# The down projection of a decoder layer: 16 of its 22 row tiles by Strassen's method with seven products

## The chip, the core and the metric

The kernel runs on one core of a Trainium2 chip. A core has five engines with instruction streams of their own: TensorE (PE, matrix products into PSUM), VectorE (DVE), ScalarE (ACT), GpSimd (POOL) and SyncE (SP), which here only issues transfers. Transfers between HBM and the on-chip SBUF run on 16 DMA engines; SP and ACT feed them through hardware queues, POOL through a software queue. The metric is the device time of one execution in microseconds (us). A run is compared with runs of the kernel before on the same chip.

## The reference, cut to what matters

The layer computes attention, a state space branch, a merge and a first layer norm; all of that is untouched. Behind it comes this, for 512 tokens, a width of 1024 and an inner width of 2816 (float32):

```
h = _layer_norm(DN_ALPHA * h + mixed @ w_o[i], ln1_g[i], ln1_b[i])
up = _causal_dwconv(h @ w_up[i], conv_w[i], conv_b[i])
val, gate = up[..., :D_FF], up[..., D_FF:]
ffn = (jax.nn.silu(gate) * val) @ w_down[i]
ple = (p[i] @ w_pe[i]) * jax.nn.sigmoid(h @ w_pe_gate[i])
h = _layer_norm(DN_ALPHA * h + ffn + ple, ln2_g[i], ln2_b[i])
```

## The kernel before, in words

Every float32 operand of a large product is split into a high part (a cast to the format that TensorE takes, by ACT) and a low part (operand minus high part, by DVE). `mm3` then makes one product of three matmuls: high by high, high by low, low by high, each with a 128x128 stationary operand and up to 512 moving columns.

SBUF is managed as pages of 128 partitions by 1024 floats (4 KB each). `Pages` hands them out in the order in which they came free, so a page's new user waits for the last reader of the old one. `Weights` streams 128 weight pages through them: SP loads a raw page (`wr`), ACT makes `wh`, DVE makes `wl`, and the raw page is freed. `use(n)` makes sure that the splits are issued one page ahead and the loads three pages ahead. The code is written in program order; a scheduler then places each instruction on its engine's queue, and the queues run strictly in order.

`ffn_up` runs over 22 feature tiles `f`. For each it makes two groups of 24 matmuls (value and gate, banks `up`), ACT and DVE apply the convolution (`cv`, one ACT activation and two DVE operations for each), ACT the SiLU, DVE the product, and the result is split into a page `act{f}`.

`ffn_down` multiplies these 22 pages by the 22 pages of `w_down`. Its eight banks (4 token tiles by 2 halves of 512 columns) accumulate over the first 16 row tiles in an order in which each weight page serves 24 matmuls. For the last 6 row tiles the order is by bank, so that each token tile ends in turn, is added to the residual `res`, normalized and stored while TensorE is at the next one.

Of the kernel before, what the change touches and what calls it, by code (L numbers as in the profile page):

```python
# [29 lines left out]
NPAGES, NHALVES = 37, 6  # L30
NPAGES_LATE = 11
LAG_B, LAG_C = 5, 7
# [52 lines left out]
class Weights:  # L85


    def __init__(self, tc, pages, srcs, fetch_ahead=FETCH_AHEAD, split_ahead=SPLIT_AHEAD):
# [5 lines left out]
    @staticmethod  # L94
    def cuts(n):
        return [slice(0, 512), slice(512, 1024)] if n == 0 else [slice(0, 1024)]

# [70 lines left out]


class Layer:  # L170
    def __init__(self, tc, cst, pages, banks, a):
        self.tc, self.nc, self.cst, self.pages, self.banks, self.a = tc, tc.nc, cst, pages, banks, a
        srcs = []

        def add(name):
            base = len(srcs)
            ap = a[name]
            srcs.extend(ap[i] for i in range(ap.shape[0]))
            return base

        self.wuv = add("w_uv")
        self.wqk = add("w_qk")
# [7 lines left out]
        self.wdn = add("w_down")  # L190
        self.W = Weights(tc, pages, srcs)


# [46 lines left out]
    def constants(self):  # L240
        nc, cst = self.nc, self.cst
        self.small_idx = {}
        self.small_buf = cst.tile([P, 28, 16], F32, name="small_buf")
        self.pair_idx = {}
        self.pair_buf = cst.tile([P, 16, 2, 16], F32, name="pair_buf")
# [9 lines left out]
        self.tri = cst.tile([P, 2, P], F32R, name="tri")  # L255
# [5 lines left out]
        self.mask = cst.tile([P, 2, P], F32R, name="mask")  # L261
# [323 lines left out]
    def ssm_load(self):  # L585
# [4 lines left out]
        for g in range(2):  # L590
            nc.sync.dma_start(self.lst[64 * g:64 * g + 64], a["log_step"][g:g + 1].to_broadcast([64, 16]))
        self.d32 = self.cst.tile([32, 16], F32, name="d32")
        nc.sync.dma_start(self.d32, a["d"])
# [10 lines left out]

        self.dec = [self.cst.tile([P, 2, P], F32, name=f"dec{i}") for i in range(2)]
        for dec in self.dec:
            nc.gpsimd.memset(dec[:, :, 0:1], 0.0)
        self.Tf = [self.cst.tile([P, 4, P], F32, name=f"Tf{i}") for i in range(2)]
        for tf in self.Tf:
# [59 lines left out]
    def ssm_prep(self):  # L669
# [13 lines left out]

        self.dd = self.cst.tile([32, 16, 32], F32, name="dd")
        self.tt_wide(self.dd, self.ident[0:32, 0:32].unsqueeze(1).to_broadcast([32, 16, 32]),
# [307 lines left out]

    def bcast_load(self, name, tag):
        pg = self.pages.get(tag)
        self.nc.gpsimd.dma_start(pg.t, self.a[name].to_broadcast([P, DM]))
        return pg
# [123 lines left out]
    def ffn_up(self):  # L1121
        nc = self.nc
        self.act = []
        for f in range(NF):
# [16 lines left out]
            yp.free()  # L1141
            self.act.append(pg)
            yield
        for pg in self.hT:
            pg.free()

    def load_conv(self):
# [4 lines left out]


    def ffn_down(self):
        nc, W = self.nc, self.W
        g2 = self.bcast_load("ln2_g", "g2")
        b2 = self.bcast_load("ln2_b", "b2")
        bk = {(t, h): self.banks.get(f"d{t}{h}") for t in range(4) for h in range(2)}
        KO = NF - 6
        for k in range(KO):  # L1160
            w = W.use(self.wdn + k)
            for t in range(4):
                for h in range(2):
                    self.token_mms(bk[t, h], self.act[k], t, h, w, k, k == 0, False)
            W.free(self.wdn + k)
            self.act[k].free()
        ws = [W.use(self.wdn + k) for k in range(KO, NF)]
        halves = (slice(0, 512), slice(512, 1024))

        q = slice(768, 1024)  # L1170
        self.tt(self.res[3].t[:, q], self.res[3].t[:, q], bk[3, 1].t[:, 256:512], ALU.add)
        for t in range(4):
            r = self.res[t].t
            parts = [(c, bk[t, i].t, False) for i, c in enumerate(halves)]
            if t == 3:
                parts[1:] = [(slice(512, 768), bk[3, 1].t[:, 0:256], False), (q, bk[0, 0].t[:, 0:256], True)]
            st, mv = self.ln_tiles(len(parts))
            ts_ = slice(t * P, t * P + P)
            for i, (c, bank, fresh) in enumerate(parts):
                for k in range(KO, NF):  # L1180
                    a, w = self.act[k].t, ws[k - KO]
                    self.mm3(bank, a[:, 0, ts_], a[:, 1, ts_], w[0].t[:, c], w[1].t[:, c],
                             fresh and k == KO, k == NF - 1)
                self.tt(r[:, c], r[:, c], bank, ALU.add)
# [114 lines left out]
def layouts(i):  # L1299
# [18 lines left out]
        "w_up": up,  # L1318
        "w_down": _rows(i["w_down"][0], 1),
        "a_re": state(i["ssm_a_re"][0]),  # L1320
# [32 lines left out]
```

## Time and profile before

| what | value |
|---|---|
| median of 3 runs | 802.91 us (802.33 to 803.2) |
| profiled execution: its time | 802.31 us |
| profiled execution: its span, first to last instruction | 800.6 us |
| time around the span (difference) | 1.71 us |
| mean granted TensorE clock | 0.997 of full speed |

The profile is of one execution. Its span is what the trace's rows add up to; the device time holds 1.71 us more. Times of a row count from the start of the span.

### The profile page before, as it was taken

Reading aid. Unit: us, or ns where it says so; the run is one execution under the profiler, and the core shown is the slowest. Engines: PE = TensorE matmul, PEld = TensorE weight load, DVE = VectorE, ACT = ScalarE, POOL = GpSimd, SP = SyncE. Lnnn points to the kernel's source line nnn. Section 1 sums busy time; section 2 is a strip of 40 time slices with the busy share of each in tenths; the row PEclk is TensorE's granted clock in tenths of the full one; section 3 lists DMA queues with packets and bytes.
Section 4 is the critical chain, followed back from the end, with each engine's and each line's share of the span. In section 5 each row is a group of like instructions: output and inputs, shape, how many; then the busy total and the mean of one; then the engine's idle time right before and its main releaser. Section 6 shows DMA issues by size and latency. Waiting matters only on the chain.

```text
span 800.6 us, 9760 instructions
## 1 busy us (share of the span) xinstructions
PE 784.6 (98%) x3716; PEld 655.8 (82%) x3716; DVE 508.2 (63%) x881; ACT 333.1 (42%) x538; POOL 24.2 (3%) x67
## 2 busy tenths in 40 slices
PE   9999999999999999999999999999999999999996
PEld 7887888878888878888888888888888888888885
DVE  6957997695767868857644665565555565432056
ACT  7435667553433375415323443444344345312000
POOL 0000000000000010013300000000000000000000
PEclk9999999999999999999999999999999999999998
DMA  8913221033122475515203322312222126431002
GB/s 319 379 70 103 56 80 54 27 107 131 35 71 91 173 237 170 187 42 180 80 27 132 106 79 79 105 52 94 93 79 79 53 90 252 158 105 53 1 27 79
DMA packets 29870, 86.73 MB, mean 108 GB/s; under 512 B 4224, under 2 KB 8448, under 8 KB 29568
## 3 DMA queue, kind: packets, MB, share of 16 engines
q1 hardware_dynamic: 27952, 80.35, 29.5%
q0 software_dynamic: 1296, 4.72, 1.6%
q10 hardware_dynamic: 576, 1.05, 0.3%
q8 instruction: 29, 0.48, 0.2%
q14 instruction: 17, 0.14, 0.0%
HBM read 79.81 MB, written 3.15 MB: 104 GB/s over the span
## 4 chain that ended last, share of the span: by engine, by line
PE 92%; DVE 3%; ACT 2%; DMA 2%; issue 1%; SPq 1%; DVEq 0%; ACTq 0%
PE up L195 30%; PE d L195 15%; PE g L195 10%; PE o L195 5%; PE pg L195 5%; PE mx L195 4%; PE z L195 3%; PE u L195 3%; PE v L195 3%; PE kb L195 2%; PE qb L195 2%; PE A L195 2%; PE pe L195 1%; PE y L195 1%; DMA y<-yst 1%; PE av L195 1%
## 5 line engine op out<-in xcount | busy, mean ns | idle before, releaser
L120 DVE TENSOR_TENSOR wl<-wr,wh 128x1024 fp32r<-128x1024 f32 (+1 forms) x129 | 155.1, 1214 | 100.0 <-ACT wh L119 82.6
L195 PE MATMUL up<-hT,wh 128*128 128x512 f32 x704 | 216.7, 389 | 0.0
L119 ACT CAST wh<-wr 128x1024 fp32r<-128x1024 f32 (+1 forms) x129 | 133.3, 1043 | 149.8 <-PE d L195 38.1
L195 PEld LDWEIGHTS up<-hT,wh 128*128 128x128 f32 x704 | 132.2, 188 | 27.5
L195 PE MATMUL up<-hT,wl 128*128 128x512 f32 x352 | 136.9, 389 | 0.0
L195 PE MATMUL d<-wh,act 128*128 128x512 f32 (+1 forms) x364 | 109.1, 382 | 0.0
L225 DVE SCALAR_TENSOR_TENSOR cv<-up,cw,cv 128x511 f32<-128x511 f32 x88 | 65.8, 748 | 32.2 <-ACT cv L1133 30.7
L195 PE MATMUL g<-xs,wh 128*128 128x512 f32 x256 | 81.0, 397 | 0.0
L195 PEld LDWEIGHTS d<-wh,act 128*128 128x128 f32 x364 | 67.6, 188 | 13.3
L195 PEld LDWEIGHTS up<-hT,wl 128*128 128x128 f32 x352 | 66.1, 188 | 13.6
L195 PE MATMUL d<-wl,act 128*128 128x512 f32 (+1 forms) x182 | 69.5, 382 | 0.0
L1133 ACT ACTIVATE cv<-up,cb,cw 128x512 f32<-128x512 f32 x44 | 34.2, 778 | 58.5 <-PE up L195 58.5
L195 PEld LDWEIGHTS g<-xs,wh 128*128 128x128 f32 x256 | 46.2, 188 | 8.6 <-issue 0.6
L195 PE MATMUL g<-xs,wl 128*128 128x512 f32 x128 | 50.0, 391 | 0.0
L195 PE MATMUL mx<-yts,wh 128*128 128x512 f32 x128 | 39.2, 390 | 1.4 <-DVE yts L903 1.4
L195 PE MATMUL pg<-wh,hT 128*128 128x512 f32 x128 | 40.1, 390 | 0.0
L195 PE MATMUL o<-wh,mx 128*128 128x512 f32 x128 | 40.0, 390 | 0.0
L195 PEld LDWEIGHTS d<-wl,act 128*128 128x128 f32 x182 | 34.2, 188 | 6.6
L216 DVE TENSOR_TENSOR cv<-cv 128x512 f32<-128x512 f32 x22 | 15.2, 692 | 24.6 <-ACT cv L232 24.6
L195 PEld LDWEIGHTS mx<-yts,wh 128*128 128x128 f32 x128 | 24.0, 188 | 6.7 <-DVE yts L903 1.8
L216 DVE TENSOR_TENSOR x<-x,d 128x512 f32<-128x512 f32 (+1 forms) x10 | 6.1, 606 | 35.1 <-PE d L195 35.1
L195 PEld LDWEIGHTS g<-xs,wl 128*128 128x128 f32 x128 | 24.0, 188 | 5.2
(180 smaller groups left out, 1143.3 us busy)
## 6 DMA issues: line engine op xcount, KB each, us to landing
wr<-in_w_up_dram SPq DMA_DIRECT2D x44, 512.0 KB, 3.3
wr<-in_w_down_dram SPq DMA_DIRECT2D x22, 512.0 KB, 3.4
wr<-in_w_g_dram SPq DMA_DIRECT2D x16, 512.0 KB, 3.3
wr<-in_w_qk_dram SPq DMA_DIRECT2D x8, 512.0 KB, 11.3
wr<-in_w_glu_dram SPq DMA_DIRECT2D x8, 512.0 KB, 4.3
wr<-in_w_o_dram SPq DMA_DIRECT2D x8, 512.0 KB, 3.9
wr<-in_w_pe_gate_dram SPq DMA_DIRECT2D x8, 512.0 KB, 3.3
wr<-in_w_uv_dram SPq DMA_DIRECT2D x7, 512.0 KB, 7.7
```

The costliest lines, as they stand in the source:

```text
L119: self.nc.scalar.copy(hi.t[:, c], raw.t[:, c])
L120: self.nc.vector.tensor_tensor(out=lo.t[:, c], in0=raw.t[:, c], in1=hi.t[:, c].bitcast(F32), op=ALU.subtract)
L195: ins = self.nc.tensor.matmul(out=out, lhsT=lhsT, rhs=rhs, start=start, stop=stop, skip_group_check=True).ins
L216: return self.nc.vector.tensor_tensor(out=out, in0=a, in1=b, op=op).ins
L225: self.nc.vector.scalar_tensor_tensor(out=out, in0=a, scalar=s, in1=b, op0=op0, op1=op1)
L1133: nc.scalar.activation(y, bank.t, AF.Identity, scale=cw[:, 2:3], bias=cb)
```

## The change

The first 16 of the 22 row tiles of `w_down` are taken as two block rows (even and odd tiles), the 1024 output columns as two block columns, and the 512 tokens as two block rows of the activations. The four blocks of this product are made by seven block products instead of eight (Winograd's form of Strassen's method), each over 8 row tiles, 2 token tiles and 512 columns: 48 matmuls. The last 6 row tiles stay as they were, through a `Weights` stream of their own (`WD`).

The activation sums are made by DVE in `ffn_up` (`combine`, tiles of 256 tokens); four of the seven left operands are split there, and three (`S1`, `A12`, `S4`) are kept as sums and split in `ffn_down` (`split_left`). The weight sums are made in `Products`: a block page is loaded by SP (16 pages), negated in place by ACT, and a second block is added by a transfer from HBM that accumulates into the page (`accum_op`), issued by POOL. Of the 28 pages (7 products by 4), the pages 4 to 7, 8 to 11, 12 to 15 and 16 to 19 need such a step; pages 8 to 11 are made from 4 to 7 and 12 to 15 from 8 to 11, in the same buffers (`dr4` to `dr7`), and 16 to 19 from `dr0` to `dr3`. Then `dh` (ACT) and `dl` (DVE) are split from the page as before. A page of weights now serves 12 matmuls.

Around it: the late page pool has 14 pages instead of 11 (tables of the state space branch move to a pool that is closed by then), and the loads of `ln2_g` and `ln2_b` move from POOL's queue to SP's.

```diff
-NPAGES_LATE = 11
+NPAGES_LATE = 14
+NS = 8
...
+class Products:
+    ORDER = (("11", None, 0),
+             ("22", None, "12"),
+             ("-T3", 1, "11"),
+             ("T2", 2, "21"),
+             ("11", 0, "12"),
+             ("21", None, 0),
+             ("22", None, 0))
+    KEPT = (0, 1, 2)
+    def __init__(self, tc, pages, blocks, fetch_ahead=5, split_ahead=1):
...
+    def fetch_to(self, n):
+        while self.nf < min(n, self.n):
+            q, j = divmod(self.nf, self.per)
+            name, of, plus = self.ORDER[q]
+            if of is None:
+                pg = self.pages.get(f"dr{self.nf}")
+                self.nc.sync.dma_start(pg.t, self.block(name, j))
+            else:
+                pg = self.raw.pop((of, j))
+            if plus:
+                self.nc.scalar.mul(pg.t, pg.t, -1.0)
+                self.nc.gpsimd.dma_start(pg.t, self.block(plus, j), accum_op=ALU.add)
+            self.raw[q, j] = pg
+            self.nf += 1
+    def split_to(self, n):
...
+            self.nc.scalar.copy(hi.t, raw.t)
+            self.nc.vector.tensor_tensor(out=lo.t, in0=raw.t, in1=hi.t.bitcast(F32), op=ALU.subtract)
+            if q not in self.KEPT:
+                self.raw.pop((q, j)).free()
...
@@ ffn_up
-            self.tt(yp.t[:, 0], yp.t[:, 0], yp.t[:, 1], ALU.mult)
-            pg = self.pages.get(f"act{f}", F32R, (P, 2, T))
-            self.split(pg.t[:, 0], pg.t[:, 1], yp.t[:, 0])
+            if f < 2 * NS:
+                self.combine(f, yp)
...
+            if f >= NF - 2:
+                self.WP.split_to(f - NF + 3)
+                self.WP.fetch_to(f - NF + 4)
@@ combine (odd tile of a pair)
+        self.tt(a12, y0[:, first], y1[:, first], ALU.mult)
+        self.tt(sq[:, 3], y0[:, last], y1[:, last], ALU.mult)
+        self.tt(sq[:, 1], a21, sq[:, 0], ALU.subtract)
+        self.tt(s1, a21, sq[:, 3], ALU.add)
+        self.tt(sq[:, 2], s1, sq[:, 0], ALU.subtract)
+        self.tt(s4, a12, sq[:, 2], ALU.subtract)
+        for i in range(2):
+            pg = self.pages.get(f"sa{p}{i}", F32R, (P, 2, 2, T // 2))
+            src = sq[:, 2 * i:2 * i + 2]
+            nc.scalar.copy(pg.t[:, :, 0], src)
+            self.tt(pg.t[:, :, 1], src, pg.t[:, :, 0].bitcast(F32), ALU.subtract)
@@ ffn_down
-        for k in range(KO):
-            w = W.use(self.wdn + k)
-            for t in range(4):
-                for h in range(2):
-                    self.token_mms(bk[t, h], self.act[k], t, h, w, k, k == 0, False)
+        def product(q, bank, a, fresh, side=lambda j: None):
...
+                for k in range(2):
+                    p = 2 * j + k
+                    for m in range(2):
+                        ts_ = slice(m * P, m * P + P)
+                        self.mm3(bank[m].t, a[p][0][:, ts_], a[p][1][:, ts_], hi[:, k], lo[:, k],
+                                 fresh and p == 0, p == NS - 1)
...
+        product(0, X, now(0, 0), True)
+        add(X, 0, 0)
+        product(1, Y, now(0, 1), True)
+        add(Y, 1, 1)
+        product(2, X, now(1, 0), False)
+        add(X, 1, 0)
+        a = left("S1")
+        product(3, Y, now(1, 1), False)
+        product(4, X, a, False)
+        add(X, 1, 1)
+        product(5, V, left("A12"), True)
+        product(6, X, left("S4"), False, lambda j: WD.use(j))
```

Three places of the built programs matter for what follows. The first is ACT's queue where the up projection ends and the down projection begins. In the kernel before it holds, beside the last convolution (`cv21`), SiLU and the split of `act21`, only casts of weight pages:

```order
L1133 ACTIVATE cv21_5466<-up211_5501,cb_314,cw_313 128x512
L119 CAST wh109_5612<-wr109_5556 128x1024
L119 CAST wh112_5702<-wr112_5646 128x1024
L232 ACTIVATE cv21_5466<-cv21_5466 128x512
L119 CAST wh110_5642<-wr110_5586 128x1024
L212 CAST act21_5537<-cv21_5466 128x512
```

In the changed kernel the same stretch reads as follows (L207 is the negation, L219 the cast of a weight page):

```order
L219 CAST dh3_5650<-dr3_5608 128x1024
L1200 ACTIVATE cv21_5534<-up211_5567,cb_314,cw_313 128x512
L207 ACTIVATE dr6_5634<-dr6_5634 128x1024
L207 ACTIVATE dr7_5654<-dr7_5654 128x1024
L207 ACTIVATE dr3_5608<-dr3_5608 128x1024
L207 ACTIVATE dr4_5610<-dr4_5610 128x1024
L299 ACTIVATE cv21_5534<-cv21_5534 128x512
L207 ACTIVATE dr5_5614<-dr5_5614 128x1024
L279 CAST act21_5597<-cv21_5534 128x512
L219 CAST dh6_5710<-dr6_5634 128x1024
L219 CAST dh2_5630<-dr2_5604 128x1024
L219 CAST dh7_5728<-dr7_5654 128x1024
```

The cast of page 2 (`dh2`), which product 0 takes third, now stands behind five negations, the SiLU, the split of `act21` and the cast of page 6 (`dh6`), which needs that page's accumulating transfer.

The second place is POOL's queue. Before, its last two entries are the loads of `ln2_g` and `ln2_b`:

```order
L996 DMA g2_5540<-in_ln2_g_dram 128x1024
L996 DMA b2_5542<-in_ln2_b_dram 128x1024
```

Now it ends with the 16 accumulating transfers, of which these are the second to the tenth:

```order
L208 DMA dr1_5532<-in_w_down_blocks_dram 128x1024
L208 DMA dr6_5634<-in_w_down_blocks_dram 128x1024
L208 DMA dr7_5654<-in_w_down_blocks_dram 128x1024
L208 DMA dr3_5608<-in_w_down_blocks_dram 128x1024
L208 DMA dr4_5610<-in_w_down_blocks_dram 128x1024
L208 DMA dr5_5614<-in_w_down_blocks_dram 128x1024
L208 DMA dr6_5634<-in_w_down_blocks_dram 128x1024
L208 DMA dr2_5604<-in_w_down_blocks_dram 128x1024
L208 DMA dr4_5610<-in_w_down_blocks_dram 128x1024
```

So pages 1 and 3 (used only as pages 17 and 19, in product 4) are summed ahead of or between the pages of product 1.

The third place is SP's queue behind the last page of `w_up`. Before, 22 pages of `w_down` follow in it; now eight block pages do, with `dr6` and `dr7` ahead of `dr4` and `dr5`, then the two loads that left POOL:

```order
L203 DMA dr2_5604<-in_w_down_blocks_dram 128x1024
L203 DMA dr3_5608<-in_w_down_blocks_dram 128x1024
L203 DMA dr6_5634<-in_w_down_blocks_dram 128x1024
L203 DMA dr7_5654<-in_w_down_blocks_dram 128x1024
L203 DMA dr4_5610<-in_w_down_blocks_dram 128x1024
L203 DMA dr5_5614<-in_w_down_blocks_dram 128x1024
L1063 DMA b2_5842<-in_ln2_b_dram 128x1024
L1063 DMA g2_5840<-in_ln2_g_dram 128x1024
```

## Rows read from the trace of the kernel before

**Rows 1.** The page, parts 1 and 2: busy time by engine; transfer rate in 40 slices.

```profile
PE 784.6 (98%) x3716; PEld 655.8 (82%) x3716; DVE 508.2 (63%) x881; ACT 333.1 (42%) x538; POOL 24.2 (3%) x67
...
GB/s 319 379 70 103 56 80 54 27 107 131 35 71 91 173 237 170 187 42 180 80 27 132 106 79 79 105 52 94 93 79 79 53 90 252 158 105 53 1 27 79
```

**Rows 2.** The chain that ended last, from 640 us: start, length, what, count.

```profile
639.96 32.87 PE up L195 x145
672.83 119.92 PE d L195 x546
...
796.74 0.66 DVEq L1349
```

**Rows 3.** TensorE's matmuls from 672 us by shape: count, busy, mean ns.

```profile
L195 PE MATMUL d<-wh,act 128*128 128x512 f32 x340 | 104.8, 389 | 0.0
L195 PE MATMUL d<-wl,act 128*128 128x512 f32 x170 | 66.1, 389 | 0.0
```

**Rows 4.** Busy time by stretch: length, busy (instructions) by engine, clock, DMA, GB/s.

```profile
450.00:665.00 215.00, 215.00 (x951) 178.07 (x950) 125.40 (x154) 88.22 (x115) 1.13 (x2) 1.00 0.25 85
665.00:740.00 75.00, 75.00 (x333) 62.12 (x332) 30.51 (x29) 25.96 (x28) 0.00 (x0) 1.00 0.41 144
```

**Rows 5.** Who waited for whom from 660 us: in total, times, longest.

```profile
ACT wh L119 <- PE d L195: 38.1, 9, 4.6
```

**Rows 6.** ACT by line and shape, whole span: count, busy, mean ns, idle before.

```profile
L119 ACT CAST wh<-wr 128x1024 fp32r<-128x1024 f32 x127 | 132.0, 1050 | 148.0 <-PE d L195 38.1 <-DMA wr<-in_w_up_dram 18.2 <-PE o L195 15.6
L1133 ACT ACTIVATE cv<-up,cb,cw 128x512 f32<-128x512 f32 x44 | 34.2, 778 | 58.5 <-PE up L195 58.5
L232 ACT ACTIVATE cv<-cv 128x512 f32<-128x512 f32 x22 | 13.9, 631 | 26.8 <-DVE cv L225 26.8
L212 ACT CAST act<-cv 128x512 fp32r<-128x512 f32 x22 | 13.7, 621 | 15.2 <-DVE cv L216 15.2
...
L232 ACT ACTIVATE gate<-gate 128x1024 f32<-128x1024 f32 x8 | 7.8, 1046 | 0.0
```

**Rows 7.** DVE by line and shape, whole span: count, busy, mean ns.

```profile
L120 DVE TENSOR_TENSOR wl<-wr,wh 128x1024 fp32r<-128x1024 f32 x127 | 153.7, 1222 | 99.0 <-ACT wh L119 81.7 <-PE d L195 9.3 <-PE up L195 7.6
...
L216 DVE TENSOR_TENSOR cv<-cv 128x512 f32<-128x512 f32 x22 | 15.2, 692 | 24.6 <-ACT cv L232 24.6
...
L216 DVE TENSOR_TENSOR vx<-pq 128x256 f32<-128x256 f32 x16 | 6.1, 422 | 0.1
```

**Rows 8.** DMA issues by line: count, KB each, median us from issue to landing.

```profile
wr<-in_w_down_dram SPq DMA_DIRECT2D x22, 512.0 KB, 3.4
...
x<-in_x_dram POOLq DMA_DIRECT2D x4, 512.0 KB, 5.4
...
praw<-in_pT_dram POOLq DMA_DIRECT2D x1, 512.0 KB, 11.9
```

**Rows 9.** Timeline of POOL, 275 to 300 us: start, length, what, count.

```profile
279.21 2.29 POOL L1010 DMA_DIRECT2D x<-in_x_dram  x4 [3.83 <-DVE yts L216]
...
282.53 0.53 POOL L1016 DMA_DIRECT2D praw<-in_pT_dram  x1
```

**Rows 10.** Landing of the four transfers into `x` on POOL's queue.

```profile
DMA to landing us min/median/max: 3.8/5.4/7.4
```

**Rows 11.** TensorE's longest waits in the whole span: in total, times, longest.

```profile
PE z L195 <- ACT wp L232: 2.0, 3, 1.6
PE mx L195 <- DVE yts L903: 1.4, 1, 1.4
```

**Rows 12.** Busy time by stretch at the very end, columns as in rows 4.

```profile
793.00:796.00 3.00, 0.00 (x0) 0.00 (x0) 2.79 (x10) 0.29 (x1) 0.00 (x0) 1.00 0.00 0
796.00:800.60 4.60, 0.00 (x0) 0.00 (x0) 1.41 (x2) 0.00 (x0) 0.00 (x0) 0.55 0.30 114
```

More of the change, by code (lines that the diff above doesn't have):

```diff
@@ L92, in __init__, with cuts @@
         self.nf = self.ns = 0
-    @staticmethod
-    def cuts(n):
-        return [slice(0, 512), slice(512, 1024)] if n == 0 else [slice(0, 1024)]
+    def cuts(self, n):
+        return [slice(0, 512), slice(512, 1024)] if n == 0 and self.halved else [slice(0, 1024)]
     def fetch_to(self, n):
@@ L189, in __init__ @@
         self.wup = add("w_up")
-        self.wdn = add("w_down")
         self.W = Weights(tc, pages, srcs)
+        self.WD = Weights(tc, pages, [a["w_down"][i] for i in range(NF - 2 * NS)], halved=False)
+        self.WP = Products(tc, pages, a["w_down_blocks"])
     def mm(self, out, lhsT, rhs, start, stop):
@@ L1122, in ffn_up @@
         nc = self.nc
-        self.act = []
+        self.act, self.left, self.now = [], {}, ([], [])
         for f in range(NF):
@@ L1145, in ffn_up, with combine @@
             pg.free()
+    def combine(self, f, yp):
+        nc, p = self.nc, f // 2
+        first, last = slice(0, T // 2), slice(T // 2, T)
+        y0, y1 = yp.t[:, 0], yp.t[:, 1]
+        if f % 2 == 0:
+            self.sq = self.pages.get(f"sq{p}", F32, (P, 4, T // 2))
+            self.tt(self.sq.t[:, 0], y0[:, first], y1[:, first], ALU.mult)
+            self.tt(y0[:, last], y0[:, last], y1[:, last], ALU.mult)
+            self.even = yp
+            return
+        sq, q = self.sq.t, p % 4
+        if q == 0:
+            for name in ("S1", "A12", "S4"):
+                self.left.setdefault(name, []).append(self.pages.get(f"{name}{p}", F32, (P, 4, T // 2)))
+        s1, a12, s4 = (self.left[name][-1].t[:, q] for name in ("S1", "A12", "S4"))
+        a21 = self.even.t[:, 0, last]
+        self.tt(a12, y0[:, first], y1[:, first], ALU.mult)
+        self.tt(sq[:, 3], y0[:, last], y1[:, last], ALU.mult)
+        yp.free()
+        self.tt(sq[:, 1], a21, sq[:, 0], ALU.subtract)
+        self.tt(s1, a21, sq[:, 3], ALU.add)
+        self.even.free()
+        self.tt(sq[:, 2], s1, sq[:, 0], ALU.subtract)
[5 more added lines that the diff above has]
+            self.tt(pg.t[:, :, 1], src, pg.t[:, :, 0].bitcast(F32), ALU.subtract)
+            self.now[i].append(pg)
+        self.sq.free()
     def load_conv(self):
@@ L1151, in load_conv, with split_left @@
         self.nc.sync.dma_start(self.cb, self.a["conv_b"])
-    def ffn_down(self):
[L1155 to L1159, printed above, removed]
-        for k in range(KO):
-            w = W.use(self.wdn + k)
-            for t in range(4):
-                for h in range(2):
-                    self.token_mms(bk[t, h], self.act[k], t, h, w, k, k == 0, False)
-            W.free(self.wdn + k)
-            self.act[k].free()
-        ws = [W.use(self.wdn + k) for k in range(KO, NF)]
-        halves = (slice(0, 512), slice(512, 1024))
-        q = slice(768, 1024)
-        self.tt(self.res[3].t[:, q], self.res[3].t[:, q], bk[3, 1].t[:, 256:512], ALU.add)
+    def split_left(self, name):
+        out = []
+        for raw in self.left.pop(name):
+            for i in range(2):
+                pg = self.pages.get(f"sl{name}{i}", F32R, (P, 2, 2, T // 2))
+                src = raw.t[:, 2 * i:2 * i + 2]
+                self.nc.scalar.copy(pg.t[:, :, 0], src)
+                self.tt(pg.t[:, :, 1], src, pg.t[:, :, 0].bitcast(F32), ALU.subtract)
+                out.append(pg)
+            raw.free()
+        return out
@@ L1172, in ffn_down @@
         for t in range(4):
[L1173 to L1176, printed above, removed]
+            r, parts = res[t], parts_of[t]
             st, mv = self.ln_tiles(len(parts))
@@ L1179, in ffn_down @@
             for i, (c, bank, fresh) in enumerate(parts):
-                for k in range(KO, NF):
-                    a, w = self.act[k].t, ws[k - KO]
+                for k in range(KD):
+                    a, w = self.act[k].t, ws[k]
                     self.mm3(bank, a[:, 0, ts_], a[:, 1, ts_], w[0].t[:, c], w[1].t[:, c],
-                             fresh and k == KO, k == NF - 1)
+                             fresh and k == 0, k == KD - 1)
                 self.tt(r[:, c], r[:, c], bank, ALU.add)
```

95 lines of the change are left out of this document (81 added, 14 removed).

## The prediction, made before the changed kernel ran

> **What bounds the kernel now.** I read the busy shares first: TensorE is busy for 784.6 of 800.6 us, DVE for 508, ACT for 333 [rows 1]. The chain that ended last says the same of the end of the program: from 640 us it runs on TensorE alone, 145 matmuls of the up projection in 32.87 us and all 546 of the down projection in 119.92 us, without a piece of another engine between them [rows 2]. One 128x512 matmul therefore takes 32.87/145 = 0.2267 us (the 389 ns of the rows by shape are a matmul's length in the pipe, not its distance to the next [rows 3]). Check: 510 of the 546 have 512 columns [rows 3], 115.6 us; the other 36, of 256 columns, take the remaining 4.3. Beside TensorE in the up projection DVE is busy for 125 and ACT for 88 of 215 us, in the first 75 us of the down projection for 31 and 26 [rows 4], and ACT waits there for pages that TensorE still holds [rows 5]: weights are early, never late. So removed matmuls are worth their full time, and anything that makes a weight page late is a loss of its full size.
>
> **What is removed.** 16 row tiles by 8 banks by 3 are 384 matmuls; seven products by 48 are 336. 48 x 0.2267 = **10.9 us less**. The shapes stay, so nothing is lost per matmul. The last six tiles and the norm behind them are as before.
>
> **What is added at no cost.** In `ffn_up`, for two feature tiles, DVE had two products and two splits of 512 columns, 4 x 0.69 = 2.8 us; now four products and four sums of 256 columns at 0.42 and two splits: 4.8 us [rows 7]. The 2 us lie in 21.8 us of TensorE work in which DVE is 58% busy. Without that cover they would cost 16 us in all. The 12 casts of `S1`, `A12`, `S4` (0.62 each on ACT, 0.69 on DVE) lie in products 2 to 6. There a page still needs only 1.05 us of ACT and 1.22 of DVE [rows 6, 7] in 12 x 0.2267 = 2.72 us of TensorE; with six pages of the plain stream beside product 6, DVE has some 15 us of splits in products 6 and the 10.9 us before it, and raw pages are there early, as no sum delays them. I take products 4 to 6 at no stall. The different order in earlier stages (three more pages) I take at nothing; the one wait of that region that could move is 1.4 us long [rows 11], so it is worth 1.4 us either way at most.
>
> **What is added on the path: late pages.** A page that is a sum needs, in order: a load, a negation (ACT, 1.05, as the in-place activation of the same size [rows 6]), an accumulating transfer on POOL's queue, a cast, a split. The trace has no accumulating transfer. Below: it is no slower than a plain one on POOL's queue, 3.8 us from issue to landing when first in line [rows 10], of which 0.53 is the issue [rows 9], 1.38 the 512 KB (524 kB) at the 379 GB/s of the busiest slice [rows 1], and 1.9 the rest. Above: the slowest plain one landed after 11.9 us, seventh in a row [rows 8, 9]. A sum reads both the block and the page, twice the bytes for the same bytes written; I take an estimate between the ends, nearest to the first in line: 2 x 1.38 = **2.76 us of the DMA engines and 5.2 us from issue to landing**.
>
> Now the queues, with 0 at the end of the last up matmul; TensorE wants page n at 2.72 n.
>
> *Page 2.* ACT casts page 3 (to 0.5), does the last convolution (0.78, to 1.3), negates pages 6, 7, 3 (to 4.4). Raw page 4 can only be issued at 0, when the last up matmul frees its page; raw 7 and the sum into page 1 are ahead of it, and it lands at 6.2 instead of 3.4. Negation 4 ends at 7.3, SiLU (0.63) 7.9, negation 5 9.0, the cast of `act21` (0.62) 9.6. Next in ACT's queue is the cast of page 6. Its transfer was issued at 2.4; the engines do sum 1 (to 2.9), raw 4 and 5 (to 5.7), sum 6 (to 8.4), and it lands 1.9 later, at 10.4. Cast 6 ends at 11.4, cast 2 at 12.5; TensorE wanted it at 5.4. **7.1 us**, and 1.0 more for the low part, which DVE starts only then (1.22 less one matmul). *Together 8.1.*
>
> *Pages 4, 5.* Sums 7, 3, 4, 5 follow at 2.76 each: sum 4 lands at 18.6, cast at 19.7, low part at 20.9; TensorE stands at page 4 at 10.9 + 8.1 = 19.0. Waits of 0.8, 0.8, and 0.3 at page 5. *1.9.*
>
> *Page 8* is the second sum in buffer 4. Its negation waits in ACT's queue for cast 5 (22.5), ends at 23.5; its transfer has the sums 6 and 2 and the load of `ln2_b` ahead, lands at 31.1, cast 32.1; TensorE is there at 31.8. 0.4 and 1.1. *1.5.*
>
> *Page 12*, the third sum: negated at 37.6 behind casts 8 to 10, lands at 42.9, cast by 44.6 behind another negation and a cast; TensorE is there at 44.2; the low part stands behind a split and two bank additions on DVE. 0.5 and 1.9. *2.4.*
>
> Sum: -10.9 + 8.1 + 1.9 + 1.5 + 2.4 = **+3.0 us**. The span of the profiled execution becomes 803.6, its time, with 1.71 around it, **805.3 us**; that execution lay 0.6 under the median of the three runs, 802.91.
>
> The price of an accumulating transfer is also stated by the Trainium skill, "Collectives: The Full Stack", section "The bandwidth ceiling: the fold count and why AG ≠ RS ≠ AR": an add on the DMA engines needs two source reads, and what lands per second falls to about half (a ratio of 1.93 there); no run here shows it yet. By it the engine time would be 2.66 and the sum about +2.5.
>
> **Rivals.**
>
> *The sums land like plain transfers* (1.38 us of the engines, 3.8 to landing). Then only page 2 stalls: raw 4 lands at about 5, cast of `act21` at 8.4, cast 6 at 9.5, cast 2 at 10.5, so 5.1 + 1.0, and pages 4 to 15 are in time. -10.9 + 6.1 = -4.8: **797.5 us, faster**. For it: of a landing of 3.8 us only 1.4 is the moving of bytes, and the second read may lie beside the first. Against: the 16 engines were nearly full where they moved 379 GB/s, so a second read has no room of its own. It decides below about 2.2 us of engine time per sum, where the sum of the walk crosses zero. The page-2 stall stays in any case, since ACT's queue alone puts cast 2 at 10 or later: more than 5 us of gain is hard to see.
>
> *The transfers become the bound.* From 2.4 on, 14 sums stand in a row until page 15. At 3 x 1.38 = 4.1 us each the last lands at 62, split 2.3 later; TensorE would like page 15 at 40.8: 23.7 of waits, +13, and up to +20 with the gaps in which POOL waits for ACT. **815 to 823 us.** For it: the seven plain transfers into `x` and behind it landed between 283.0 and 294.4, 1.9 us apart even without an add [rows 8 to 10]; twice that is 3.8. Against: other loads ran beside them.
>
> *The clock falls in the stall.* No wait of TensorE in this trace is longer than 1.6 us [rows 11], and its granted clock is 1.00 in the stretches before; after the last matmul it was still 1.00 for 3 us and 0.55 in the next 4.6 [rows 12], that is, it had gone from 2.4 to 1.2 GHz. A 7 us stall at page 2 could do that. One page at 1.2 GHz costs 2.7 us, two 5.4, of which the 1.9 at pages 4 and 5 are given back: +0.8 to +3.5 on top, **806 to 809 us**. The Trainium skill, "TensorE: Matmul & The Clock Gate", section "What's actually happening", says that idleness takes the clock to the lower of two levels and activity releases it, which the end of this trace agrees with (0.55).
>
> **How the numbers follow.** The likeliest, sums at about twice a plain transfer: 0.45, its own range 801.5 to 812 (2.2 to 3.2 us a sum, 1.4 us of order elsewhere). The same with the lower clock: 0.1. Plain speed: 0.25. Transfer-bound: 0.2. 0.2% is 1.6 us here, about what runs of this kernel can tell from no change. Faster holds all of the plain case and little else, 0.26; same, 801.3 to 804.5, is the lower part of the likeliest case, 0.14; slower 0.60. The range reaches from the plain case to the far end of the bound one: 797 to 823.
>
> **What would show it.** In the profile after: 3,668 PE matmuls in place of 3,716; a wait of TensorE for the cast `dh` of 5 to 9 us about 5.4 us into the down projection, with the cast of page 6 waiting for its transfer just ahead; short waits at pages 4, 8 and 12; none in products 4 to 6. An accumulating transfer's landing near 5 us when alone and up to 10 in a row. The prediction is wrong if these land under 4 us or over 8 when alone, if `dh2` does not wait, or if waits appear in products 4 to 6, where I allow none.

## Result and the profile after

| | before | after |
|---|---|---|
| median (9 runs each, same chip) | 802.92 us (802.33 to 804.69) | 808.91 us (807.08 to 814.05) |
| ratio | 1 | 1.0077 [1.0056, 1.0098] |
| profiled execution: time, span | 802.31, 800.6 us | 807.08, 805.3 us |

Slower by 6 us where +3.0 (805.3 us) was forecast, inside the range of 797 to 823. The profiled execution is the fastest of its nine: what the others waited for in the 2 us more of the median, no trace shows. Their mean granted clock is on record, though: 0.987 to 0.992, against 0.994 in the profiled one. A thousandth of the clock is, by estimate, 1.6 us at the lower level (0.001 x 805 / 0.5), so the others spent some 3 to 11 us more there: that speaks for longer or more waits of TensorE in them than the trace below shows. (The ratios in this document leave out one execution of 1304 us, with the casts in page order, and one of 2017 us, with plain transfers on POOL, which the medians still hold.)

The page of the changed kernel, parts 1 and 3 (queue, kind: packets, MB, share of 16 engines' span):

```profile
PE 778.2 (97%) x3668; PEld 648.7 (81%) x3668; DVE 547.0 (68%) x960; ACT 366.8 (46%) x578; POOL 38.5 (5%) x81
...
q0 software_dynamic: 3312, 12.06, 6.8%
```

TensorE has 48 matmuls and 6.4 us of busy time less than in [rows 1]. The chain that ended last ran on TensorE without a break from 640 us on in [rows 2]; now it does so only from here on, behind a low part that DVE delivers:

```profile
721.19 63.99 PE p L262 x281
```

TensorE's waits in the whole span (in total, times, longest; the counterparts are [rows 11]):

```profile
PE p L262 <- ACT dh L219: 7.3, 2, 7.1
PE mx L262 <- DVE yts L970: 2.4, 1, 2.4
...
PE u L262 <- DVE xs L361: 1.8, 1, 1.8
PE p L262 <- DVE dl L220: 1.5, 3, 0.8
```

Where they lie in the down projection, from TensorE's timeline (start, length, what, [idle before <- releaser]). Product 0 starts at 676.75 us:

```profile
681.97 0.39 PE L262 MATMUL p<-dh,sa 128*128 128x512 f32 x1
689.50 1.22 PE L262 MATMUL p<-dh,sa 128*128 128x512 f32 x2 [7.15 <-ACT dh L219]
690.95 0.79 PE L262 MATMUL p<-dl,sa 128*128 128x512 f32 x1 [0.23 <-DVE dl L220]
...
708.25 0.50 PE L262 MATMUL p<-dh,sa 128*128 128x512 f32 x1 [0.19 <-ACT dh L219]
709.51 0.50 PE L262 MATMUL p<-dl,sa 128*128 128x512 f32 x1 [0.76 <-DVE dl L220]
...
721.19 0.50 PE L262 MATMUL p<-dl,sa 128*128 128x512 f32 x1 [0.49 <-DVE dl L220]
```

The first two pages run at the old pace and end at 682.2, 5.4 us into the down projection. Page 2 waits until 689.5 and then starts slowly: two matmuls take 1.22 us and not 0.62. Page 8 (708) and page 12 (721) wait a little; behind it nothing waits. Windows around page 2 (length, PE busy, granted clock, DMA share, GB/s):

```profile
682.00:686.00 4.00, 0.35 (x2) 1.00 1.05 257
686.00:689.00 3.00, 0.00 (x0) 0.52 1.07 212
689.00:693.00 4.00, 3.27 (x7) 0.50 1.07 211
693.00:696.00 3.00, 3.00 (x15) 1.00 1.05 209
```

With TensorE idle from 682.2 on, the granted clock was 1.00 until 686 and then 0.5 (1.2 GHz), up to 693. From 689.50 to 693.12 seven matmuls started; at 0.2267 each they would take 1.59 us, so with the wait of 0.23 there are 1.8 us more (the expectations below still put the clock at 3). Not all of this is the clock's. The third matmul needs page 2's low part, which DVE finished at 690.90, as the second of two in this row:

```profile
688.54 2.36 DVE L220 TENSOR_TENSOR dl<-dr,dh 128x1024 fp32r<-128x1024 f32 x2 [0.70 <-ACT dh L219]
```

At the upper clock the first two would have been issued by 689.95, and TensorE would have waited for it to 690.95, 1.0 us. So, as an estimate, the late page cost 7.3 us (682.2 to 689.5), the late low part 1.0, and the clock the last 1.0. The same windows show the DMA engines full while they move 210 GB/s, half of what plain transfers move in the trace of the single transfers below (401). What ACT did in the wait:

```profile
678.98 2.94 ACT L207 ACTIVATE dr<-dr 128x1024 f32<-128x1024 f32 x3
682.32 1.06 ACT L207 ACTIVATE dr<-dr 128x1024 f32<-128x1024 f32 x1 [0.40 <-DMA dr<-in_w_down_blocks_dram]
683.28 0.61 ACT L299 ACTIVATE cv<-cv 128x512 f32<-128x512 f32 x1
685.55 1.06 ACT L207 ACTIVATE dr<-dr 128x1024 f32<-128x1024 f32 x1 [1.66 <-DMA dr<-in_w_down_blocks_dram]
686.51 0.60 ACT L279 CAST act<-cv 128x512 fp32r<-128x512 f32 x1
687.46 1.99 ACT L219 CAST dh<-dr 128x1024 fp32r<-128x1024 f32 x2 [0.34 <-DMA dr<-in_w_down_blocks_dram]
```

These are the negations of pages 6, 7, 3, of 4 and of 5 (each of the last two waits for its raw load), the split of `act21`, then the casts of pages 6 and 2 in one row. Landing of the 16 accumulating transfers in us, min/median/max:

```profile
DMA to landing us min/median/max: 5.3/7.9/11.2
```

So the down projection, 120.1 us before, is 120.9 us: -10.9, +9.3 at page 2 (page, low part and clock), +1.5 at page 8 and +0.8 at page 12, which is the +0.8 to within 0.1. The last two are read as the distances of the matmuls there less 0.2267 each. The start of the down projection moved by +4.1 us (672.66 to 676.75), the tail by -0.2: together the 4.7 of the spans. So in this execution most of the loss lies ahead of the down projection, where the forecast had none, and the down projection itself lost 0.8 us where it had 3.0.

### The profile page after: what moved, and what is told of

It reads as the page before. It is cut to its first block, busy times and chain, and to the rows that moved or that the text cites. A ratio compares the mean times of both kernels' runs of the same rounds, so it can differ in the third digit from the quotient of the medians.

```text
span 805.3 us, 9856 instructions
## 1 busy us (share of the span) xinstructions
PE 778.2 (97%) x3668; PEld 648.7 (81%) x3668; DVE 547.0 (68%) x960; ACT 366.8 (46%) x578; POOL 38.5 (5%) x81
## 5 line engine op out<-in xcount | busy, mean ns | idle before, releaser
L121 DVE TENSOR_TENSOR wl<-wr,wh 128x1024 fp32r<-128x1024 f32 (+1 forms) x113 | 135.7, 1212 | 59.5 <-ACT wh L120 43.2
L120 ACT CAST wh<-wr 128x1024 fp32r<-128x1024 f32 (+1 forms) x113 | 116.8, 1043 | 90.6 <-PE o L262 13.4
L220 DVE TENSOR_TENSOR dl<-dr,dh 128x1024 fp32r<-128x1024 f32 x28 | 33.7, 1222 | 24.5 <-ACT dh L219 24.5
L262 PE MATMUL p<-dh,sa 128*128 128x512 f32 x128 | 41.2, 400 | 7.3 <-ACT dh L219 7.3
L219 ACT CAST dh<-dr 128x1024 fp32r<-128x1024 f32 x28 | 28.5, 1046 | 15.6 <-DMA dr<-in_w_down_blocks_dram 15.6
L262 PEld LDWEIGHTS p<-dh,sa 128*128 128x128 f32 x128 | 24.6, 193 | 13.1 <-ACT dh L219 8.2
L208 POOL DMA_DIRECT2D dr<-in_w_down_blocks_dram x16 | 13.9, 869 | 311.4 <-ACT dr L207 311.1
L262 PEld LDWEIGHTS pg<-wh,hT 128*128 128x128 f32 x128 | 24.0, 188 | 4.9
```

The costliest lines, as they stand in the source:

```text
L120: self.nc.scalar.copy(hi.t[:, c], raw.t[:, c])
L121: self.nc.vector.tensor_tensor(out=lo.t[:, c], in0=raw.t[:, c], in1=hi.t[:, c].bitcast(F32), op=ALU.subtract)
L208: self.nc.gpsimd.dma_start(pg.t, self.block(plus, j), accum_op=ALU.add)
L219: self.nc.scalar.copy(hi.t, raw.t)
L220: self.nc.vector.tensor_tensor(out=lo.t, in0=raw.t, in1=hi.t.bitcast(F32), op=ALU.subtract)
L262: ins = self.nc.tensor.matmul(out=out, lhsT=lhsT, rhs=rhs, start=start, stop=stop, skip_group_check=True).ins
```

## Experiments

Changes are the ratio to the kernel before on the same chip, less one, times 802.9 us.

| kernel | median us | ratio [95%] | change us |
|---|---|---|---|
| the change | 808.91 | 1.0077 [1.0056, 1.0098] | +6.2 |
| sums left out | 793.99 | 0.9885 [0.9872, 0.9898] | -9.2 |
| before with 14 pages | 805.02 | 1.0017 [1.0001, 1.0033] | +1.4 |
| plain transfers on POOL | 802.78 | 0.9981 [0.9961, 1.0] | -1.5 |
| filler in the wait | 812.02 | 1.0098 [1.0075, 1.0121] | +7.9 |
| casts in page order | 809.06 | 1.0069 [1.0056, 1.0082] | +5.5 |
| four sums held back | 809.73 | 1.0072 [1.0048, 1.0097] | +5.8 |
| plain product second | 809.73 | 1.0091 [1.006, 1.0122] | +7.3 |
| plain second, all in order | 818.03 | 1.0177 [1.0152, 1.0202] | +14.2 |
| sums on DVE | 799.47 | 0.9951 [0.9938, 0.9964] | -3.9 |
| sums on DVE, pages late | 798.02 | 0.9934 [0.9919, 0.9949] | -5.3 |
| sums on DVE, pages late, by need | 799.95 | 0.9967 [0.9954, 0.998] | -2.6 |

### What each part costs

**The sums left out.** All 28 pages come plainly over SP.

```diff
-            if of is None:
+            if True:
...
-            if plus:
-                self.nc.scalar.mul(pg.t, pg.t, -1.0)
-                self.nc.gpsimd.dma_start(pg.t, self.block(plus, j), accum_op=ALU.add)
...
-    KEPT = (0, 1, 2)
+    KEPT = ()
```

> All 28 weight pages are loaded plainly by SP; the negations and the accumulating transfers are left out, so seven products are made of unsummed blocks. Both theories: no wait of TensorE in the products. What is open is the start of the down projection, which was 4.1 us later than before in the profile of the change: if the change's order in earlier stages costs that, median 795 to 797; if it was that execution's own first transfers, 791 to 793 (802.9 less 10.9).

-9.2 us, and its profile has no wait of TensorE in the products: its down projection takes 109.2 us (676.16 to 785.35), 10.9 less than the 120.1 before. The median of 793.99 lies between the two expected bands: something of the change's surroundings costs, but less than 4.1.

**Before with 14 pages.** The page count, the tables and the loads of `ln2_g` and `ln2_b` of the change, in the old kernel.

```diff
-NPAGES_LATE = 11
+NPAGES_LATE = 14
...
-        g2 = self.bcast_load("ln2_g", "g2")
+        g2 = self.bcast_load("ln2_g", "g2", nc.sync)
```

> The kernel before with only the change's surroundings: 14 late pages in place of 11, the tables in the pool that closes, the loads of ln2_g and ln2_b on SP. If these cost the 4.1 us ahead of the down projection: first product at 7.1 in place of 5.0 us, the wait for yts 2.4 in place of 1.4, median 804 to 807. If the first 2 us were that execution's own: first product near 5.0 and median 802.5 to 804.

+1.4 us (0.1 to 2.6), and its down projection takes 120.1 us as before, so the loss lies ahead of it. The median is in the band of the first theory, and the first product of this profile came at 7.2 us as that theory had it. Its wait for `yts`, whole span:

```profile
PE mx L195 <- DVE yts L903: 2.7, 1, 2.7
```

With three more pages SP's queue holds a weight page ahead of 16 small loads that `yts` needs, and this wait was 1.9 to 3.4 us in the ten profiles with 14 pages from the start, against 1.4 [rows 11]. That the pages make it longer is likely, not shown: in the kernel of the single transfers below, with 11 pages and the old order of these loads, the wait was 2.4.

```profile
PE mx L195 <- DVE yts L903: 2.4, 1, 2.4
```

2.1 us of the changed kernel's shifted start come with its first matmul. The first matmul of `u` comes at 5.0 to 5.4 us in 11 of the 14 profiles of this study and at 7.1 or 7.2 in three (the change, this kernel and the filler), with the same instructions ahead of it; seven of the ten profiles with 14 pages have it early, so the pages alone do not make it late. Whether they make it likelier, three of ten against none of four cannot tell.

**Plain transfers on POOL.**

```diff
-                self.nc.gpsimd.dma_start(pg.t, self.block(plus, j), accum_op=ALU.add)
+                self.nc.gpsimd.dma_start(pg.t, self.block(plus, j))
```

> The changed kernel with the 16 transfers of POOL as plain ones: same queue, bytes, negations and order, and the block overwrites the page in place of being added. If the add is what costs (2.8 us of the engines against 1.4): raw pages land earlier, pages 4 to 12 no longer wait, the page-2 wait stays at 3 to 5 us by ACT's queue, median 798 to 803. If the queue and the negations cost and not the add: median 806 to 809.

-1.5 us. Its page (queue row as above), and TensorE's waits in the down projection:

```profile
q0 software_dynamic: 3312, 12.06, 4.3%
```

```profile
PE p L262 <- ACT dh L219: 7.4, 1, 7.4
PE p L262 <- DVE dl L220: 0.2, 1, 0.2
```

Pages 4 to 12 no longer wait, and page 2 waits as long as with the adds, longer than the 3 to 5 us expected. The program order on ACT and POOL is the same, so the adds do not make that wait; ACT's order does, with raw loads that its negations wait for. The down projection takes 118.8 us here and 120.9 with the adds: 2.1 us between the two profiles, against 7.7 between the two ratios (+6.2 and -1.5, each known to within 1.7 us either side). The slower executions of the changed kernel, of which no trace exists, must hold the rest. The queue took 4.3% of 801.5 us here and 6.8% of 805.3 there, for the same packets: 20.3 us more for 16 adds, 1.27 us each. That queue's 23 transfers took 34.5 us plainly, 1.50 each; a sum is then 2.77 us, and 2.76 was the estimate.

**One transfer by itself.** In the up projection of the kernel before, where DMA is a quarter busy:

```diff
...
+            elif f == 3:
+                self.nc.gpsimd.dma_start(pg.t, src[8 + i])
+            elif f in (5, 7):
+                self.nc.gpsimd.dma_start(pg.t, src[16 + f + i], accum_op=ALU.add)
+            elif f == 9:
+                self.nc.gpsimd.dma_start(pg.t, src[24 + i], accum_op=ALU.add)
...
```

> The kernel before with transfers of 512 KB on POOL's queue into spare pages during the up projection, where DMA is a quarter busy: six plain ones in a row, one plain alone, two accumulating ones alone, six accumulating in a row, six plain in a row; the data is used by nobody. By the prediction's estimate: plain alone 3.8 us from issue to landing, accumulating alone 5.2 us; in a row, 1.4 us more for each plain one and 2.8 us for each accumulating one. By the rival of the prediction (adds land like plain ones): no difference. Time as before, 801 to 804.

Its one execution took 804.9 us, 0.9 more than expected. Landing of the plain one alone, of the two accumulating ones (each alone), and of six accumulating ones in a row:

```profile
DMA to landing us min/median/max: 3.5/3.5/3.5
...
DMA to landing us min/median/max: 5.1/6.1/7.0
...
DMA to landing us min/median/max: 5.1/10.3/15.2
```

Windows while plain ones move (464 to 470) and while accumulating ones do (length, POOL busy, clock, DMA share, GB/s):

```profile
464.00:470.00 6.00, 0.61 (x2) 1.00 1.00 401
...
554.00:563.00 9.00, 0.00 (x0) 1.00 1.06 209
```

The engines are full in both and move 401 and 209 GB/s, 1.92 to 1. So 512 KB take 1.31 us plainly and 2.51 added. The Trainium skill, "Collectives: The Full Stack", section "The bandwidth ceiling: the fold count and why AG ≠ RS ≠ AR", has a ratio of 1.93 between a collective that copies and one that adds; this trace, with 1.92, agrees.

**The clock.** Thirty matmuls into a bank that nobody reads, ahead of page 2:

```diff
+                if n == 2:
+                    spare = self.banks.get("spare")
+                    for i in range(30):
+                        self.mm(spare.t, a[0][0][:, 0:P], ...)
```

> The changed kernel with 30 more matmuls of 512 columns (6.8 us at the higher clock) into a bank that nobody reads, just ahead of page 2's: TensorE works through the wait. Theory (the clock is a price of its own): the granted clock stays at 1.00 behind the wait, and the 3 us of the lower clock come off: median 805 to 807. Rival (transfers): pages 4 to 12 wait for their sums as much longer: median 808 to 810.

+7.9 us, beyond the rival's band. Two windows, and the waits from 665 us:

```profile
680.00:688.00 8.00, 7.95 (x36) 1.00 1.04 236
688.00:696.00 8.00, 6.49 (x26) 1.00 1.07 213
```

```profile
PE p L262 <- DVE dl L220: 3.7, 5, 1.4
PE p L262 <- ACT dh L219: 3.2, 3, 1.8
```

The clock stayed at 1.00 until 712 us, page 2 itself waited 0.83 us behind the filler, and the waits behind it grew. But the run does not settle what the clock is worth. Page 2 came no sooner (13.24 us behind the start of product 0, against 12.75 in the changed kernel), and the largest of the later waits has another cause:

```profile
713.64 0.73 PE L262 MATMUL p<-dh,sa 128*128 128x512 f32 x2 [1.83 <-ACT dh L219]
```

This is page 9, with 1.4 us more for its low part. With the extra matmuls in the program the scheduler set ACT's queue differently: the cast of page 9 stands behind those of pages 10 and 11, four splits of `S1` and a negation, where in the changed kernel it follows the cast of page 8. Without these 3.2 us the change would be near +4.7 us by estimate, below the changed kernel's +6.2. A filler with ACT's order held was not run.

### Does another order help?

**Casts in page order.**

```diff
-            self.nc.scalar.copy(hi.t, raw.t)
+            cast = self.nc.scalar.copy(hi.t, raw.t).ins
+            if self.last is not None:
+                self.after(cast, self.last)
+            self.last = cast
```

> The casts of weight pages are kept in page order on ACT, so the cast of page 2 no longer stands behind that of page 6 and behind the negation of page 5; nothing else changes. Theory (ACT's order): what TensorE loses in the down projection is the page-2 wait (7.1 us) and the lower clock behind it (some 3 us). Page 2's cast then follows the negation of page 4 and the split of act21: wait 2 to 4 us, little or no time at half clock, the later waits stay below 3 us together, median 802 to 805. Rival (transfers): from product 0 to product 3 the DMA engines are full with 16 sums of about 2.8 us each, so what is saved at page 2 is waited for at pages 4 to 12: those waits rise from 1.7 to 5 us or more, median 807 to 810.

The rival. Waits in the down projection:

```profile
PE p L266 <- ACT dh L219: 6.2, 3, 3.4
PE p L266 <- DVE dl L223: 2.7, 5, 0.8
```

Page 2 waits 2.5 us with its low part, no longer 7.4, and the sum of all waits is 8.9 as it was 8.8: 3.4 at page 4, the rest in small pieces up to page 12. In this kernel and in the changed one the DMA engines are full (a share of 0.97 and 1.03) from 672 to 712 us. The sum into page 4 landed some 11 us behind its issue (678.8 to 689.7), and the cast waited for it. Two things weaken the reading. The scheduler set the negations and the splits of `S1` anew as well (the sums into pages 10 and 19 moved back), so the casts are not all that changed. And the down projection takes 125.7 us, 4.7 more than in the changed kernel's profile with the same waits: TensorE also ran at the lower clock twice (a mean of 0.63 from 688 to 696 us, 0.79 from 720 to 728).

**Four sums held back** (pages 16 to 19, on top of the casts in order):

```diff
-                self.nc.scalar.mul(pg.t, pg.t, -1.0)
+                neg = self.nc.scalar.mul(pg.t, pg.t, -1.0).ins
+                if of == 0:
+                    self.after(neg, self.last)
```

> Like the kernel with the casts in page order (809.1 us), and the sums of pages 16 to 19, which product 4 needs last, are held back until page 12 is cast, so that four transfers of 2.8 us leave the stretch in which the DMA engines are full. Theory (transfers): this takes up to 8.4 us (three sums; the first lay in idle time) from what pages 4 to 12 wait for; waits of TensorE in the down projection fall from 8.9 to 3 to 5 us, median 800 to 804. Rival (ACT's order): only three negations of 1.05 us leave ACT's queue; median 806 to 809.

No gain. POOL's timeline, and windows of the same stretch:

```profile
682.99 0.86 POOL L210 DMA_DIRECT2D dr<-in_w_down_blocks_dram  x1 [0.61 <-ACT dr L207]
697.34 2.75 POOL L210 DMA_DIRECT2D dr<-in_w_down_blocks_dram  x3 [13.48 <-ACT dr L207]
```

```profile
688.00:696.00 8.00, 7.47 (x29) 0.92 0.57 122
696.00:704.00 8.00, 8.00 (x37) 1.00 0.77 161
```

The engines are no longer full from 688 to 704 us (from 704 to 712 they are again, 1.06), so that far the expectation was right, but the waits, 9.4 us, and the time stayed: behind the first four sums POOL issues nothing for 13.5 us, since the next sums go into the same four buffers. Each needs the cast, the low part and a negation of the page before it, and then some 8.9 us (median) to land. A buffer's next page comes 11 to 13 us after the one before, and TensorE uses up four pages in 10.9.

**The plain product second** (product 5, A12 by block 21):

```diff
-             ("22", None, "12"),
-             ("-T3", 1, "11"),
...
+             ("21", None, 0),
+             ("22", None, "12"),
+             ("-T3", 2, "11"),
```

> Product 5 (A12 by the plain block 21, four pages without a sum) runs second, so the products with summed pages come 48 matmuls (10.9 us) later; the same products and sums otherwise. Theory (ACT's order and little time for the sums): fewer negations stand ahead of page 2's cast, and every sum has 10.9 us more; waits in the down projection fall from 8.8 to under 3 us and the clock stays at its higher level, median 796 to 800. Rival (transfers): four more plain pages (4 x 1.4 us) are loaded in the same stretch, the engines stay full, waits of 4 to 8 us come at pages 8 to 16, median 801 to 806.

Missed on both sides: +7.3 us. The scheduler also set page 4 ahead of page 2 on TensorE. ACT's timeline:

```profile
687.53 1.06 ACT L207 ACTIVATE dr<-dr 128x1024 f32<-128x1024 f32 x1 [4.19 <-DMA dr<-in_w_down_blocks_dram]
688.49 1.97 ACT L219 CAST dh<-dr 128x1024 fp32r<-128x1024 f32 x2
```

Here the negation of page 8 stands ahead of page 2's cast and waits for its raw load: TensorE waited 5.8 us for page 2, whose cast needs no sum. **With every cast and negation in program order and four sums held back:**

```diff
+                if self.last is not None:
+                    self.after(neg, self.last)
```

> The plain product second, the casts in page order, no negation ahead of a cast that the program issues before it, and the sums of pages 20 to 23 (as 16 to 19 before) held back. Theory (transfers and ACT's order together): product 1's sums have 10.9 us more and no other sums ahead of them; waits below 3 us, clock at its higher level, median 795 to 799, faster than both kernels. Rival (the engines stay full whatever the order: 12 sums of 2.8 us for pages 8 to 19 against 2.72 us of TensorE a page, and ten plain loads): waits of 4 to 8 us, median 801 to 806.

Far off: +14.2 us. Windows early and late in the products:

```profile
680.00:688.00 8.00, 5.52 (x17) 0.81 0.42 154
688.00:696.00 8.00, 8.00 (x36) 0.98 0.71 149
736.00:744.00 8.00, 4.96 (x20) 1.00 1.06 274
744.00:752.00 8.00, 4.31 (x9) 0.65 1.05 275
```

The DMA engines are partly idle at first (the first sum is issued only at 686.5 us, since the negations stand behind the casts), and are full when the sums held back, the last raw pages and `w_down` come together.

### The sums on DVE

```diff
-                self.nc.scalar.mul(pg.t, pg.t, -1.0)
-                self.nc.gpsimd.dma_start(pg.t, self.block(plus, j), accum_op=ALU.add)
+                other = self.pages.get(f"ds{self.nf}")
+                self.nc.sync.dma_start(other.t, self.block(plus, j))
+                self.nc.vector.tensor_tensor(out=pg.t, in0=other.t, in1=pg.t, op=ALU.subtract)
+                other.free()
```

> The changed kernel with the 16 sums made on DVE: the second block is loaded plainly by SP into a page of its own (1.4 us of the engines) and DVE subtracts (1.22 us); negations and accumulating transfers are gone, the result is the same. Theory (the chain in a buffer): with accumulating transfers each step from a cast to the next page in the same buffer takes 12 to 14 us against 10.9 us of TensorE, and the first three negations stand ahead of page 2; both go, waits of TensorE in the down projection under 3 us, median 795 to 799, faster than both kernels. Rival (DVE becomes the bound): 28 low parts and 16 sums of 1.22 us, the splits of S1, A12, S4 and the additions fill some 70 of 76 us of DVE, low parts come late; waits of 4 to 10 us, median 799 to 806.

-3.9 us, faster than both kernels; its median is just above the expected band. The sums still follow each other in the same four buffers; the negations, the adds' time on the DMA engines and their landing went together, so the run does not tell what each was worth. **And with the three pages handed out in the up projection:**

```diff
-        lay.pages.more(ctx.enter_context(tc.tile_pool(name="late", bufs=1)), NPAGES_LATE)
+        lay.pages.more(lay.late, 11)
...
+        self.pages.more(self.late, NPAGES_LATE - 11, 11)
         for _ in self.ffn_up():
```

> As the sums on DVE, and the three more pages are handed out only in the up projection, so that SP's queue up to there is that of the kernel before. If the three pages are what made TensorE wait longer for yts (2.4 to 3.4 us in place of 1.4) and cost the kernel with 14 pages 2 us: the wait is 1.4 again and the median 1 to 3 us below that of the sums on DVE. If not: the same median within 1 us.

-5.3 us, the best kernel of the study. Its waits, and the stretch of products 2 to 4 (length, busy time of PE, PEld, DVE, ACT, POOL, clock, DMA share, GB/s):

```profile
PE p L265 <- ACT dh L222: 3.0, 1, 3.0
...
PE mx L265 <- DVE yts L973: 1.4, 1, 1.4
...
PE p L265 <- DVE dl L223: 0.5, 1, 0.5
```

```profile
696.00:744.00 48.00, 48.00 (x214) 39.75 (x213) 47.90 (x51) 29.24 (x35) 0.00 (x0) 1.00 0.67 246
```

The wait for `yts` is 1.4 again. The two intervals overlap, so the 1.4 us between these kernels is likely, and not sure. DVE works without a gap for 48 us and TensorE does not wait for it. **By need:** loads in the order of use, and product 0's additions on DVE behind the low part of page 6.

```diff
+        ins = self.nc.sync.dma_start(out, src).ins
+        if self.loaded is not None:
+            self.after(ins, self.loaded)
...
+        product(1, Y, now(0, 1), True, lambda j: add(X, 0, 0, WP.low) if j == 1 else None)
```

> As the sums on DVE with the three pages handed out late (798.0 us), and two orders set by need: SP loads the blocks in the order in which the pages are used, and the additions of product 0's banks on DVE come behind the low part of page 6. In the profile without this TensorE waited 3.0 us for page 4, whose cast needed a page that DVE's sum of page 5 frees; that sum stood behind the two additions, which wait for TensorE. Theory: the wait and the lower clock behind it go (3.5 and about 1.5 us), waits in the down projection under 1 us, median 793 to 796. Rival (DVE is full from 688 to 744 us anyway): the gain comes back as waits for low parts in products 2 to 4; median 797 to 799.

Worse than without, -2.6 us, with 4.4 us of waits in the down projection where under 1 was expected. SP's timeline, and one window of this kernel and then of the one before it:

```profile
673.33 0.42 SPq L196 DMA_DIRECT2D ds<-in_w_down_blocks_dram  x1
679.43 0.33 SPq L196 DMA_DIRECT2D dr<-in_w_down_blocks_dram  x1
```

```profile
672.00:680.00 8.00, 8.00 (x37) 1.00 0.36 131
```

```profile
672.00:680.00 8.00, 8.00 (x37) 1.00 1.02 413
```

The load of page 5's block waited 5.7 us, until 679.4, for the SBUF page that DVE's split of `act21` frees, and in order all others stood behind it. In this kernel, at its limit of pages, the order in which they come free was worth more than the order of use. Two orders changed at once, so what the later additions are worth alone is not shown.

## Why the prediction was right, and where not

**What is removed** (10.9): right. Without the sums the down projection is 10.9 us shorter in the profile; by the ratios, against the kernel with 14 pages, -9.2 - 1.4 = -10.6 us.

**No cost in the earlier stages** (0, at most 1.4 either way): this term was mis-sized. The surroundings cost +1.4 (0.1 to 2.6), in the profile up to 4.1, of which 2.1 are the late first loads. The bound did not hold either: a wait of 1.4 us can shrink by no more than 1.4, but it can grow by more, and in the profile without sums it was 3.4.

**Page 2** (8.1 = 7.1 + 1.0): the right place, 5.4 us into the down projection, and the right size, 7.3 + 1.0. Of its causes, ACT's order was the one: with plain transfers the wait is the same, with the casts in page order it is 2.5. The walk had page 6's cast wait for its sum; in the trace that wait is 0.34 us, and ACT came to the cast late by itself, behind two negations that waited for raw loads. The prediction's own figure with plain transfers (5.1 + 1.0) was some 2.5 us too low (7.6 + 1.0): ACT's negations waited 3.8 us for raw loads there.

**Pages 4, 5, 8, 12** (5.8): 2.3 us in the profile, at pages 8 and 12, none at 4 and 5; the 1.0 us of lower clock ahead of them gave the sums that much more time. So the term was too high for this execution, the fastest. By the ratios the add costs 7.7 us (-1.5 to +6.2), and the prediction had 13.9 - 6.1 = 7.8 between the plain and the adding transfer; but the two profiles differ by 2.1, so that agreement is not shown to be more than chance.

**No wait in products 4 to 6**: right, to the chain of 64 us. **The price of an add**: right, 5.1 and 7.0 us to landing alone (5.2), 2.5 to 2.8 of the engines (2.76); its issue takes 0.87 us on POOL and not 0.53. "Up to 10 in a row" was 11.2, and 15.2 for six issued together.

**The rivals.** Plain landing is refuted. The clock did fall in the stall, which had 0.1, and the 807.1 us of the profiled execution lie in that rival's band of 806 to 809. But it cost 1.0 us there, and the late start brought the time into the band. What keeping it up would gain is not shown, as the filler changed ACT's order too. Transfers as the bound (815 to 823) did not show as such, but its point was nearer than the 0.2 said: the engines were full for 40 us, and the two kernels that took most of the page-2 wait away (the casts in page order, and four sums held back) waited as long in all. Both changed other orders too, so no run takes the page-2 wait away by itself; in these two, other waits came in its place.

In all, by the ratios: +6.2 = +1.4 (surroundings) - 10.6 (matmuls) + 7.7 (negations and loads on POOL, with page 2's wait) + 7.7 (adds). The terms are differences between kernels, so they add up by construction, and the last three are each uncertain by some 2 us. The closeness of the forecast is in part luck: in the profile the down projection lost 0.8 us and not 3.0, and the stages ahead of it 4.1 and not 0.

Open is what the executions slower than the profiled one waited for. The 3 us at page 4 in the best kernel can be read from its trace: the cast starts when DVE's sum of page 5 frees a page, and that sum stands behind two additions that waited 2.9 us for TensorE. What taking this wait away is worth is open too.

## What to carry to other kernels

Work taken from the busiest engine is worth what the new feeders of that engine leave of it: here 10.6 us of matmuls were paid for with 15.4 us, by the ratios, of late operands. A sum made in place, several times in one buffer, is a chain of latencies; compare the time from one page in a buffer to the next (11 to 13 us here) with the time that the consumer takes for as many pages (10.9), before the order of anything is changed. Here DVE had the time, and a plain load and a subtraction of 1.22 us there beat a negation and an accumulating transfer (-3.9 against +6.2 us). And where a scheduler places the instructions, an edit of one order moves others: compare the queues of both programs before an experiment is read.

## What the hardware showed that was not expected

The issue of an accumulating transfer holds POOL for 0.86 to 0.94 us, against 0.53 for a plain one of the same size. And the first loads of this program landed in one of two ways, some 2 us apart, with the same instructions ahead (three of 14 profiles late), which is as much as some of the changes here are worth.
